# Where a queue's loads stand, and weight sums made by the vector engine, in a hybrid decoder layer

## Chip, core and metric

The kernel runs on one core of a Trainium2 chip. The metric is device time in microseconds (us), the median over runs of the whole program. The engines are named as in the profile: PE is TensorE (matrix products; PEld are its weight loads), DVE VectorE, ACT ScalarE, POOL GpSimd, SP SyncE. SP, ACT and POOL also issue DMA transfers, each from its own in-order instruction stream.

## What is computed

One layer of a decoder over 1,104 tokens (1,040 of a prompt with its 16 meta tokens, 8 sequences of 8 more), model width 1,024. Cut to what matters here:

```
xn = rms_norm(x, gains[0])
u, gate_a, q, f, i, og, m_a, m_b = split(xn @ w_in)           # eight slabs of 1024 columns
y_a = rg_lru(conv(u)) * gelu(gate_a)                          # first recurrent branch
y_b = rms_norm(hgrn2(q, f, i)) * silu(og)                     # second recurrent branch
mixed = sigmoid(m_a) * (y_a @ w_branch_a) + sigmoid(m_b) * (y_b @ w_branch_b)
x = x + rms_norm(mixed @ w_out, gains[1])
x = x + rms_norm(square(relu(rms_norm(x, gains[2]) @ w_up)) @ w_down, gains[3])
```

## The kernel before

All products are made in 16-bit floats with a high and a low part of each operand, three matmuls in place of one. Most weights are multiplied by a seven-product scheme (Strassen-Winograd). A *pair* is two blocks of 128 output channels: 2 x 7 products (the seven for each half of the tokens, `c = 0` and `c = 1`), each of 12 matmuls of 128x272 or 128x276, 168 in all. In the order in which PE makes them the seven use the weight operands S3, S1, A11, S2, A22, S4, A12. The S are sums of the four blocks of a weight matrix; the memory holds the blocks so that each S comes by adding one block to the sum before it.

Each operand is split for use: ACT writes the high part (line 194), DVE the low part (line 196). This *preparation* of the next pair runs between the products of this one: after product i the code calls `tk(i)`, a *tick*, and at the ticks listed in PLACES (c = 0: 1, 3, 5; c = 1: 0, 2, 3, 5; in the second branch c = 0: 0, 1, 2, 3, 5) the generator of the next pair is advanced, before and after `hq.tick`, which advances queued side work after a count of ticks (a *hold*). The engines' instructions stand in exactly the order in which this code emits them.

`gen_pair` makes a pair's operands thus. SP loads blocks 1 and 2 into a tile `ws` (two such tiles, `raw_dma`, line 164) and block 0 into a tile `sa` (two such tiles, `sum_load`, line 182); POOL adds block 1 to `sa` by an accumulating DMA (line 184). The splits are S1 (`sa`), A11 (`ws`), A22 (`ws`), S2, S3, A12, S4. Between them POOL issues three more accumulating DMAs of 256 KB: line 233 (after S1, for S2), line 236 (after A11, for S3), line 242 (after S2, for S4); SP reloads half of `ws` with block 3 (line 239, for A12).

The order of the work around the change: pairs u0 to u7, then gate pairs g3 to g7, then four pairs with `w_branch_b` (the *first branch stage*, operands `ybh`, `ybl`) and four with `w_branch_a` (the *second branch stage*), then `w_out`, then the MLP. The last recurrences run beside u7 to g4. When they are done, `yb_start` hands their memory to new tiles and `y_prep` begins to load the stored parts of y_b on ACT's queue (line 1274), to split them (lines 1280, 1282) and to add them (line 1287) into seven operands numbered 0 to 6, in two halves k = 0 and k = 2; a product of the first branch that needs operand i first forces the rest of that preparation into the order (`ywait`). `th_load` (line 1374, ACT's queue) brings a stored gate slab of 1,088 KB back for a branch pair; the two tiles it uses are those from which g6 and g7 are stored (line 1334, POOL).

In `pair`, line 372 and 380 are ACT's copies after products 1 and 3; line 376 is DVE's `v + b4` after product 2, line 384 `b2 - u` after product 4, line 459 and 460 the differences after product 5. A product that accumulates in or reuses a PSUM bank waits for them: product 6 for line 376, product 2 of the next half for lines 459 and 460.

Of the kernel before, what the change touches and what calls it, by code (L numbers as in the profile page):

```python
# [68 lines left out]
def layer_kernel(ctx, tc, xT, w_pl, w_pr, w_o, w_up, w_dn, gw, par, sconv, slru, shg,  # L69
# [47 lines left out]

    def add_unit(kind, src):
        units.append(kind)
        raws.append(src[:, 1:3] if kind in ("pr", "pn") else src)  # L120
        if kind in ("pr", "pn"):
            prs.append((kind, src))

    npl = npr = 0
# [6 lines left out]
    def add_pair(kind="pr"):  # L131
        nonlocal npr
        add_unit(kind, w_pr[npr])
        npr += 1
# [9 lines left out]
    for _ in range(3):  # L144
        add_pair()
    for s in LSEQ:
        add_pair("pn" if s in NOSTR else "pr")
    for i in range(8):
        add_pair()
        if i >= 4:  # L150
            for j in range(2):
                add_unit("wo", w_o[2 * (i - 4) + j])
    for g in range(NG):
        for src in (w_up, w_dn):
            for i in range(4):
                add_unit("pr", src[4 * g + i])

    st = {"raw": 0, "unit": 0}
    rawq = []
# [8 lines left out]
    def raw_get():  # L168
        if not rawq:
            raw_dma()  # L170
        return rawq.pop(0)
# [5 lines left out]
    def sum_load():  # L177
        if nsum[0] < len(prs):
            kind, src = prs[nsum[0]]
            nsum[0] += 1  # L180
            q = asp.tile([P, 512], F32, tag="sa", name=nm("sa"))
            nc.sync.dma_start(q, src[:, 0])
            if kind == "pr":
                nc.gpsimd.dma_start(q, src[:, 1], accum_op=OP.add)
            sums.append((q, src))

# [11 lines left out]
    def prep(slot=None):  # L198
        kind = units[st["unit"]]
        st["unit"] += 1  # L200
        if slot is None:
            slot = iter(lambda: single(opp), 0)
        ops = {}

        def gen_plain():
            t0 = raw_get()
            ops[0] = next(slot)
            yield from w_split(t0[:, 0], ops[0])
            yield
            ops[1] = next(slot)  # L210
            yield from w_split(t0[:, 1], ops[1])
            raw_dma()

        def gen_wo():
            t0 = raw_get()
            yield from w_split(t0.rearrange("p b (k c) -> p (b k) c", c=P), next(slot))
            raw_dma()
            yield

        def gen_pair():  # L220
            if not sums:
                sum_load()
            q, src = sums.pop(0)
            t0 = raw_get()
            sum_load()
            a, b = t0[:, 0], t0[:, 1]

            def sp(name, x):
                ops[name] = next(slot)
                yield from w_split(x, ops[name])  # L230

            yield from sp("S1", q)
            nc.gpsimd.dma_start(q, src[:, 2], accum_op=OP.add)
            yield
            yield from sp("A11", b)
            nc.gpsimd.dma_start(b, src[:, 0], accum_op=OP.add)
            yield
            yield from sp("A22", a)
            nc.sync.dma_start(a, src[:, 3])
            yield  # L240
            yield from sp("S2", q)
            nc.gpsimd.dma_start(q, src[:, 3], accum_op=OP.add)
            yield
            yield from sp("S3", b)
            yield
            yield from sp("A12", a)
            raw_dma()
            yield
            yield from sp("S4", q)


        def gen_blocks():
            q, src = sums.pop(0)
            t0 = raw_get()
            sum_load()
            a, b = t0[:, 0], t0[:, 1]
            for name, x in (("A22", a), ("A21", q), ("A11", b), ("A12", a)):
                ops[name] = next(slot)
                yield from w_split(x, ops[name])
                if name == "A22":  # L260
                    nc.sync.dma_start(a, src[:, 3])
                if name != "A12":
                    yield
            raw_dma()

        return ops, {"pl": gen_plain, "wo": gen_wo, "pr": gen_pair, "pn": gen_blocks}[kind]()

    cur = {}

# [996 lines left out]

    def y_prep(s, scale, dst, pool, k, ready):
        ks = slice(k, k + 2)  # L1270

        def load(n, tag):
            t = pool.tile([P, 2, HW], F32, tag=f"{tag}{k}", name=nm("ys"))
            nc.scalar.dma_start(t, yb_d[s][n][:, ks])
            return t

        def split(i, t, sc, hold=1):
            hi, lo = (x[:, ks] for x in dst(i))
            yield 0, 1.2, hold
            ACT.activation(hi, t, AF.Copy, scale=sc)  # L1280
            yield 1.3, 0, 1
            DVE.scalar_tensor_tensor(lo, t, sc, hi, op0=OP.mult, op1=OP.subtract)
            ready.add((i, k))

        def add(t, x, hold):
            yield 1.3, 0, hold
            DVE.tensor_tensor(t, t, x, op=OP.add)

        yield 0, 0, 1 + k
        ta, tb = load(4, "yA"), load(3, "yB")  # L1290
        yield from split(5, ta, scale, 8)
        yield 0, 0, 2
        ta = load(0, "yA")
        yield from split(3, tb, scale)
        yield from split(0, ta, scale, 4)
        yield 0, 0, 2
        ta = load(2, "yA")
        yield from add(tb, ta, 6)
        yield from split(4, tb, scale)
        yield from split(2, ta, scale)  # L1300
        yield 0, 0, 2
        ta = load(1, "yA")
        yield from add(tb, ta, 6)
        yield from split(6, tb, scale)
        yield from split(1, ta, -scale)
# [7 lines left out]
    def yb_start():  # L1313
        yield 0, 0, 1
        while hq.has(lrus):
            yield 0, 0, 1
        nc.sync.dma_start(o_conv, convout)
        nc.sync.dma_start(o_h, hout)
        lctx.close()
        ybp = sbuf(ybctx, "ybp", 1, "right")  # L1320
        yb["ysp"] = sbuf(ybctx, "ysp")
        yb["h"] = ybp.tile([P, 7, 4, HW], F16, name="ybh")
        yb["l"] = ybp.tile([P, 7, 4, HW], F16, name="ybl")
        for k in (0, 2):
            ygens[1].append(hq.add(y_prep(1, SY, lambda i: (yb["h"][:, i], yb["l"][:, i]), yb["ysp"], k, yready[1])))

    def ywait(s, i):
        for k in (0, 2):
# [53 lines left out]

    hq.drain([e[0] for e in hq.q if e[0] not in ygens[1]])
    th_load(0)
    th_load(1)

    def ya_start():
        yield 0, 0, 1
        while hq.has(ygens[1]):
            yield 0, 0, 1  # L1390
        for k in (0, 2):
            ygens[0].append(hq.add(y_prep(0, SY / (2 * KAP), lambda i: tuple(x[:, :, :HW] for x in BYa(i)), yb["ysp"], k,
                                          yready[0])))

    for p in range(4):
        tb = ths[p]
# [40 lines left out]
        yield 0, 0, 2  # L1437
        th_load(p)

    def th_late(p):  # L1440
        yield 0, 0, 7
        th_load(p)

    APLACES = ((0, 1, 2, 3, 5), (0, 2, 3, 5))
    ac = acp.tile([P, 2, TO], F32, name="ac")
    for p in range(4):
        if p == 0:
            hq.add(th_late(5))
        if p == 3:
            nc.scalar.dma_start(ac, ac_d[3])  # L1450
        ta = ths[p + 4]
# [566 lines left out]
```

## Time and profile before

| | us |
|---|---|
| median of 3 runs | 1944.09 (1940.73 to 1944.8) |
| profiled execution, its time | 1946.51 |
| its span, first to last instruction | 1944.7 |
| PE busy | 1792.0 (92%) |
| DVE busy | 1397.6 (72%) |
| ACT busy | 998.4 (51%) |
| POOL busy | 448.2 (23%) |

The span is covered by PE for all but 153 us. In the profile's 40 slices of 48.6 us PE stands at 6 to 9 tenths from the 18th to the 27th slice (about 826 to 1313 us) and at 9 tenths in most others; the granted TensorE clock is 0.975 over the whole, and 7 tenths in one slice there. So the stage of the gate pairs and of the two branches is the place to read closely.

### The profile page before, as it was taken

The page shows a single profiled execution, that of the slowest core. Times are in us where ns is not written, and L with a number is a line of the kernel's source. Part 1 is how long each engine was busy: PE and PEld are TensorE (multiplying, and loading weights), DVE is VectorE, ACT ScalarE, POOL GpSimd, SP SyncE. Part 2 cuts the span into 40 slices and gives each one's busy share as a digit, 9 for nine tenths or more (in the row PEclk, how much of TensorE's full clock was granted, in tenths as well). Part 3 has the DMA queues.
Part 4 walks back from the last instruction along what each step waited for, and adds up shares of the span by engine and source line. Part 5 has one row for each costly group of instructions (what it writes and reads, how often), then busy time and mean ns, then how long its engine had stood idle before and what let it go on. Part 6 is the DMA issues. An engine that isn't in the chain of part 4 may idle for free. (4 is left out here: it accounts for less than half of the span.)

```text
span 1944.7 us, 43580 instructions
## 1 busy us (share of the span) xinstructions
PE 1792.0 (92%) x18000; PEld 1532.9 (79%) x18000; DVE 1397.6 (72%) x2615; ACT 998.4 (51%) x2115; POOL 448.2 (23%) x539
## 2 busy tenths in 40 slices
PE   5899999999999999988697869889999999999987
PEld 4788888898888877767476669877888888888776
DVE  7998989888864677756486546687557757756767
ACT  4555545555444666755243334566446426525653
POOL 3512121221221000121022315463111111121222
PEclk9999999999999999999799989999999999999999
DMA  5253333433444233477688853225544544454635
GB/s 177 61 111 77 90 101 80 127 85 88 103 129 123 68 96 95 91 200 201 192 257 219 195 134 93 72 64 106 118 101 103 114 114 100 109 111 102 135 73 163
DMA packets 122809, 232.40 MB, mean 120 GB/s; under 512 B 11632, under 2 KB 49392, under 8 KB 120944
## 3 DMA queue, kind: packets, MB, share of 16 engines
q0 software_dynamic: 46480, 94.88, 25.9%
q1 hardware_dynamic: 62704, 108.52, 17.2%
q10 hardware_dynamic: 13424, 26.19, 4.2%
q8 instruction: 141, 2.31, 0.5%
q14 instruction: 60, 0.49, 0.1%
HBM read 187.92 MB, written 41.63 MB: 118 GB/s over the span
## 5 line engine op out<-in xcount | busy, mean ns | idle before, releaser
L361 PEld LDWEIGHTS <-sh 128*128 128x128 f16 x3968 | 390.7, 98 | 151.8 <-issue 81.6
L362 PEld LDWEIGHTS <-sl 128*128 128x128 f16 x3968 | 390.7, 98 | 85.3 <-DVE sl L196 7.9
L359 PEld LDWEIGHTS <-sh 128*128 128x128 f16 x3968 | 391.5, 99 | 80.0 <-ACT sh L194 7.5
L359 PE MATMUL pd<-xh,sh 128*128 128x276 f16 (+1 forms) x1016 | 285.6, 281 | 12.7 <-DVE et L459 5.0
L361 PE MATMUL pd<-xl,sh 128*128 128x276 f16 (+1 forms) x1016 | 285.5, 281 | 0.0
L362 PE MATMUL pd<-xh,sl 128*128 128x276 f16 (+1 forms) x1016 | 285.3, 281 | 0.0
L359 PE MATMUL q<-aoh,sh 128*128 128x272 f16 (+2 forms) x1008 | 259.5, 267 | 8.2 <-ACT sh L194 5.3
L362 PE MATMUL q<-aoh,sl 128*128 128x272 f16 (+2 forms) x1008 | 259.5, 267 | 3.1 <-DVE sl L196 3.1
L359 PE MATMUL q<-hoh,sh 128*128 128x272 f16 (+2 forms) x952 | 255.4, 273 | 7.3 <-DVE U L1757 4.6
L196 DVE SCALAR_TENSOR_TENSOR sl<-ws,sh 128x512 f16<-128x512 f32 x282 | 193.6, 688 | 91.8 <-ACT sh L194 91.0
L361 PE MATMUL q<-aol,sh 128*128 128x272 f16 (+2 forms) x1008 | 259.5, 267 | 0.0
L362 PE MATMUL q<-hoh,sl 128*128 128x272 f16 (+2 forms) x952 | 255.4, 273 | 1.3 <-DVE sl L196 1.3
L361 PE MATMUL q<-hol,sh 128*128 128x272 f16 (+2 forms) x952 | 255.5, 273 | 0.6 <-DVE hol L1526 0.6
L359 PE MATMUL pd<-tsh,sh 128*128 128x276 f16 (+1 forms) x768 | 218.9, 285 | 30.6 <-DVE U L376 16.7
L196 DVE SCALAR_TENSOR_TENSOR sl<-sa,sh 128x512 f16<-128x512 f32 x189 | 134.1, 711 | 156.7 <-ACT sh L194 155.1
L362 PE MATMUL pd<-tsh,sl 128*128 128x276 f16 (+1 forms) x768 | 219.3, 286 | 0.0
L361 PE MATMUL pd<-tsl,sh 128*128 128x276 f16 (+1 forms) x768 | 219.1, 285 | 0.0
L194 ACT ACTIVATE sh<-ws 128x512 f16<-128x512 f32 x282 | 169.0, 621 | 70.6 <-DMA ws<-in_w_pr 31.6
L194 ACT ACTIVATE sh<-sa 128x512 f16<-128x512 f32 x189 | 117.4, 623 | 147.8 <-DMA sa<-in_w_pr 89.9
L1009 PE MATMUL pd<-sh,xh 128*128 128x128 f16 (+1 forms) x576 | 102.9, 221 | 3.0 <-ACT F L478 2.0
L1011 PE MATMUL pd<-sh,xl 128*128 128x128 f16 (+1 forms) x576 | 102.9, 221 | 0.0
L1010 PE MATMUL pd<-sl,xh 128*128 128x128 f16 (+1 forms) x576 | 102.7, 221 | 0.0
(375 smaller groups left out, 4110.3 us busy)
## 6 DMA issues: line engine op xcount, KB each, us to landing
sa<-in_w_pr POOLq DMA_DIRECT2D x87, 256.0 KB, 4.6
ws<-in_w_pr SPq DMA_DIRECT2D x35, 512.0 KB, 3.9
sa<-in_w_up POOLq DMA_DIRECT2D x48, 256.0 KB, 3.8
sa<-in_w_dn POOLq DMA_DIRECT2D x48, 256.0 KB, 3.8
ys<-yb ACTq DMA_DIRECT2D x20, 544.0 KB, 5.5
sa<-in_w_pr SPq DMA_DIRECT2D x35, 256.0 KB, 3.3
ws<-in_w_pr SPq DMA_DIRECT2D x35, 256.0 KB, 2.9
th<-th ACTq DMA_DIRECT2D x8, 1088.0 KB, 6.6
```

The source lines that it names most:

```text
L194: ACT.activation(hi, src, AF.Copy, scale=SW)
L196: DVE.scalar_tensor_tensor(lo, src, SW, hi, op0=OP.mult, op1=OP.subtract)
L359: PE.matmul(o, h[:, k, :], bh[:, k, c0:c0 + w], start=first and k == 0, stop=False, skip_group_check=not first)
L361: PE.matmul(o, h[:, k, :], bl[:, k, c0:c0 + w], start=False, stop=False, skip_group_check=not first)
L362: PE.matmul(o, l[:, k, :], bh[:, k, c0:c0 + w], start=False, stop=(k == nk - 1), skip_group_check=not first)
L1009: PE.matmul(po, a, wh[:, k % 4, :], start=(k == 0), stop=False)
L1010: PE.matmul(po, a, wl[:, k % 4, :], start=False, stop=False)
L1011: PE.matmul(po, b, wh[:, k % 4, :], start=False, stop=(k == KT - 1))
```

## The change

Two edits of place and one of method.

*Place.* `y_prep` takes its first hold as an argument: 7 ticks in place of 1 where the operands of y_b are made (the other use keeps 1). The second `th_load` is no longer issued with the first one ahead of the first branch, but 7 ticks into it.

*Method.* A new kind of preparation, `gen_half`, stands for 17 pairs: u0, u1, g3 to g7, the eight branch pairs and the first two of `w_up`. The order of splits is A22, S1, A11, S2, A12, S3, S4. The sums for S2 and S4 are DVE additions of 128x512 (lines 270 and 276 of the changed kernel); those for S1 and S3 stay accumulating DMAs on POOL (line 184, and 271 in place of 236).

```
-        raws.append(src[:, 1:3] if kind in ("pr", "pn") else src)
+        raws.append(src[:, 1:3] if kind in ("pr", "pn", "ph") else src)
...
     for s in LSEQ:
-        add_pair("pn" if s in NOSTR else "pr")
+        add_pair("pn" if s in NOSTR else "ph")
     for i in range(8):
-        add_pair()
+        add_pair("ph")
...
+                add_unit("ph" if src is w_up and g == 0 and i < 2 else "pr", src[4 * g + i])
...
-            if kind == "pr":
+            if kind != "pn":
                 nc.gpsimd.dma_start(q, src[:, 1], accum_op=OP.add)
...
+        def gen_half():
...
+            yield from sp("A22", a)
+            nc.sync.dma_start(a, src[:, 3])
+            yield
+            yield from sp("S1", q)
+            yield
+            yield from sp("A11", b)
+            DVE.tensor_tensor(q, q, b, op=OP.add)
+            nc.gpsimd.dma_start(b, src[:, 0], accum_op=OP.add)
+            yield
+            yield from sp("S2", q)
+            yield
+            yield from sp("A12", a)
+            DVE.tensor_tensor(q, q, a, op=OP.add)
+            yield
+            yield from sp("S3", b)
+            raw_dma()
+            yield
+            yield from sp("S4", q)
...
-        yield 0, 0, 1 + k
+        yield 0, 0, hold + k
...
-            ygens[1].append(hq.add(y_prep(1, SY, lambda i: (yb["h"][:, i], yb["l"][:, i]), yb["ysp"], k, yready[1])))
+            ygens[1].append(hq.add(y_prep(1, SY, lambda i: (yb["h"][:, i], yb["l"][:, i]), yb["ysp"], k, yready[1], 7)))
...
     th_load(0)
-    th_load(1)
+
+    def th_late(p, n):
+        yield 0, 0, n
+        th_load(p)
+
+    hq.add(th_late(1, 7))
```

*The first loads of y_b on ACT's queue, in pair g5.* Names: `ys<-yb14`, `ys<-yb13` are the loads, `th` the gate slab of g5, `U_1443` belongs to the second half of g5 and `U_1458` to the first half of g6 (copies of lines 372 and 380, 404 and 412 after), `sh` are the high parts of weights. Before, ACT:

```order
L518 ACTIVATE th_1428_12204<-th_1428_12204 128x276
L518 ACTIVATE th_1428_12204<-pd_1435_12243 128x276
L1274 DMA ys_1441_12344<-yb14_134 128x1088
L1274 DMA ys_1442_12346<-yb13_133 128x1088
L372 ACTIVATE U_1443_12348<-pd_1444_12349 128x276
L194 ACTIVATE sh_1445_12363<-sa_1395_11948 128x512
L1274 DMA ys_1448_12382<-yb14_134 128x1088
L1274 DMA ys_1449_12384<-yb13_133 128x1088
L380 ACTIVATE U_1443_12348<-pd_1450_12386 128x276
L194 ACTIVATE sh_1451_12400<-ws_1388_11865 128x512
```

After, ACT:

```order
L194 ACTIVATE sh_1447_12391<-ws_1388_11865 128x512
L194 ACTIVATE sh_1450_12410<-ws_1388_11865 128x512
L550 ACTIVATE th_1428_12204<-th_1428_12204 128x2x276
L194 ACTIVATE sh_1453_12444<-sa_1395_11948 128x512
L550 ACTIVATE th_1428_12204<-th_1428_12204 128x276
L1306 DMA ys_1455_12448<-yb14_134 128x1088
L1306 DMA ys_1456_12450<-yb13_133 128x1088
L550 ACTIVATE th_1428_12204<-pd_1446_12377 128x276
L404 ACTIVATE U_1458_12467<-pd_1459_12468 128x276
L1306 DMA ys_1460_12482<-yb14_134 128x1088
L1306 DMA ys_1461_12484<-yb13_133 128x1088
```

The loads moved from the middle of g5 (ahead of its copies U of c = 1) to its end, two of the four to behind the first copy U of g6.

*The start of the first branch on ACT's queue.* `th<-th0` and `th<-th1` are the gate slabs, `U_1521` (before) and `U_1518` (after) the copies of its first half pair, `ys<-yb11` the last two loads of y_b, `ybh` high parts of its operands. Before, ACT:

```order
L1274 DMA ys_1514_12923<-yb11_131 128x1088
L1280 ACTIVATE ybh_12327<-ys_1492_12741 128x1088
L518 ACTIVATE th_1489_12725<-th_1489_12725 128x2x276
L194 ACTIVATE sh_1516_12958<-sa_1463_12501 128x512
L518 ACTIVATE th_1489_12725<-th_1489_12725 128x276
L518 ACTIVATE th_1489_12725<-pd_1508_12887 128x276
L1274 DMA ys_1518_12976<-yb11_131 128x1088
L1374 DMA th_1519_12979<-th0_135 128x2176
L1374 DMA th_1520_12981<-th1_136 128x2176
L372 ACTIVATE U_1521_12983<-pd_1522_12984 128x272
L194 ACTIVATE sh_1525_13015<-sa_1494_12757 128x512
L380 ACTIVATE U_1521_12983<-pd_1527_13020 128x272
```

After, ACT:

```order
L1406 DMA th_1517_12971<-th0_135 128x2176
L404 ACTIVATE U_1518_12973<-pd_1519_12974 128x272
L194 ACTIVATE sh_1522_13006<-ws_1484_12666 128x512
L412 ACTIVATE U_1518_12973<-pd_1524_13012 128x272
L1306 DMA ys_1525_13026<-yb11_131 128x1088
L1312 ACTIVATE ybh_12326<-ys_1502_12844 128x1088
L194 ACTIVATE sh_1527_13043<-sa_1492_12749 128x512
L1312 ACTIVATE ybh_12326<-ys_1456_12450 128x1088
L1306 DMA ys_1529_13051<-yb11_131 128x1088
L1312 ACTIVATE ybh_12326<-ys_1461_12484 128x1088
L1312 ACTIVATE ybh_12326<-ys_1525_13026 128x1088
L194 ACTIVATE sh_1532_13088<-ws_1484_12666 128x512
```

The load of `th1` left the place ahead of the copies, and the two loads of `yb11` came from ahead of it to behind the second copy U, the second of them behind a split of operand 6.

*The same place on DVE:* `ys_1456<-ys_1456,ys_1525` (line 1319) adds the load of `yb11` into operand 6, line 408 and 416 are `v + b4` and `b2 - u` of the first half. After, DVE:

```order
L408 TENSOR_TENSOR U_1518_12973<-U_1518_12973,pd_1520_12989 128x272
L1314 SCALAR_TENSOR_TENSOR ybl_12327<-ys_1461_12484,ybh_12326 128x1088
L196 SCALAR_TENSOR_TENSOR sl_1523_13007<-ws_1484_12666,sh_1522_13006 128x512
L416 TENSOR_TENSOR U_1518_12973<-pd_1526_13029,U_1518_12973 128x272
L1314 SCALAR_TENSOR_TENSOR ybl_12327<-ys_1502_12844,ybh_12326 128x1088
L196 SCALAR_TENSOR_TENSOR sl_1528_13044<-sa_1492_12749,sh_1527_13043 128x512
L1319 TENSOR_TENSOR ys_1456_12450<-ys_1456_12450,ys_1525_13026 128x1088
L1314 SCALAR_TENSOR_TENSOR ybl_12327<-ys_1456_12450,ybh_12326 128x1088
L1319 TENSOR_TENSOR ys_1461_12484<-ys_1461_12484,ys_1529_13051 128x1088
L1314 SCALAR_TENSOR_TENSOR ybl_12327<-ys_1461_12484,ybh_12326 128x1088
```

Before, DVE:

```order
L376 TENSOR_TENSOR U_1521_12983<-U_1521_12983,pd_1523_12998 128x272
L196 SCALAR_TENSOR_TENSOR sl_1526_13016<-sa_1494_12757,sh_1525_13015 128x512
L1287 TENSOR_TENSOR ys_1442_12346<-ys_1442_12346,ys_1514_12923 128x1088
L384 TENSOR_TENSOR U_1521_12983<-pd_1528_13035,U_1521_12983 128x272
L196 SCALAR_TENSOR_TENSOR sl_1530_13050<-ws_1485_12673,sh_1529_13049 128x512
L1282 SCALAR_TENSOR_TENSOR ybl_12328<-ys_1442_12346,ybh_12327 128x1088
L1287 TENSOR_TENSOR ys_1449_12384<-ys_1449_12384,ys_1518_12976 128x1088
L1282 SCALAR_TENSOR_TENSOR ybl_12328<-ys_1449_12384,ybh_12327 128x1088
```

The sum of operand 6 stands at the same place in both; the load that it reads stands later on ACT's queue.

*POOL around the first pair of the second branch stage* (`sa<-in_w_pr` are lines 184, 233, 242, `ws<-in_w_pr` is line 236, 271 after, `th<-ac` merges the two branches). Before:

```order
L1378 DMA ac3_146<-th_1613_13649 128x2176
L184 DMA sa_1668_14083<-in_w_pr 128x512
L233 DMA sa_1631_13791<-in_w_pr 128x512
L236 DMA ws_1664_14049<-in_w_pr 128x512
L1418 DMA th_1648_13908<-ac0_143 128x2x272 x2
L242 DMA sa_1631_13791<-in_w_pr 128x512
L1418 DMA th_1648_13908<-ac0_143 128x2x272 x2
L184 DMA sa_1703_14342<-in_w_pr 128x512
```

After:

```order
L1410 DMA ac3_146<-th_1613_13649 128x2176
L184 DMA sa_1668_14083<-in_w_pr 128x512
L1455 DMA th_1648_13908<-ac0_143 128x2x272
L271 DMA ws_1664_14049<-in_w_pr 128x512
L1455 DMA th_1648_13908<-ac0_143 128x2x272 x3
L184 DMA sa_1703_14342<-in_w_pr 128x512
```

Of three accumulations per pair that follow the first, one is left, and one merge transfer now stands ahead of it.

## Rows read from the trace of the kernel before

**Rows 1.** Busy time by stretch; columns as in its first row.
```profile
core 0: us, PE busy (x) PEld busy (x) DVE busy (x) ACT busy (x) POOL busy (x), PEclk, DMA share, GB/s
860.00:922.00 62.00, 52.32 (x423) 41.93 (x422) 33.03 (x53) 28.22 (x52) 11.31 (x14) 0.97 0.79 227
922.00:960.00 38.00, 18.41 (x103) 12.37 (x103) 17.29 (x25) 10.62 (x17) 3.28 (x4) 0.64 0.57 166
960.00:1037.00 77.00, 71.39 (x607) 59.17 (x606) 60.35 (x98) 34.07 (x55) 12.89 (x16) 1.00 0.85 252
1037.00:1153.00 116.00, 83.99 (x661) 66.79 (x661) 66.50 (x122) 36.69 (x67) 31.81 (x32) 0.92 0.82 196
960.00:980.00 20.00, 20.00 (x175) 16.89 (x174) 14.51 (x26) 7.93 (x14) 4.00 (x5) 1.00 0.84 264
```

**Rows 2.** PE's waits, second branch stage: total, times, longest.
```profile
PE pd L359 <- DVE U L376: 16.7, 4, 5.3
PE pd L359 <- DVE th L550: 3.8, 2, 2.7
```

**Rows 3.** Line 233, 960 to 1153: who waited, and landing times.
```profile
  ACT sh L194: 45.0, 7
DMA to landing us min/median/max: 6.0/8.1/9.2
```

**Rows 4.** Line 242, same stretch: landing times.
```profile
DMA to landing us min/median/max: 3.8/5.3/8.4
```

**Rows 5.** Line 236, same stretch: landing times.
```profile
DMA to landing us min/median/max: 8.2/8.8/10.3
```

**Rows 6.** Timeline, first pair of the second branch stage: start, duration, engine, idle before.
```profile
1038.90 0.33 SPq L164 DMA_DIRECT2D ws<-in_w_pr  x1
1044.96 0.63 ACT L194 ACTIVATE sh<-ws 128x512 f16<-128x512 f32 x1 [6.55 <-DMA ws<-in_w_pr]
1046.72 0.28 PE L359 MATMUL pd<-xh,sh 128*128 128x272 f16 x1 [1.81 <-DVE et L459]
1047.42 0.86 POOL L184 DMA_DIRECT2D sa<-in_w_pr  x1 [8.82 <-DMA sa<-in_w_pr]
1048.50 1.55 POOL L236 DMA_DIRECT2D ws<-in_w_pr  x1
1056.11 0.63 ACT L194 ACTIVATE sh<-sa 128x512 f16<-128x512 f32 x1 [9.72 <-DMA sa<-in_w_pr]
1057.87 0.39 PE L359 MATMUL pd<-tsh,sh 128*128 128x272 f16 x1 [5.32 <-DVE U L376]
```

**Rows 7.** ACT's timeline around its two long waits.
```profile
869.92 0.40 ACT L372 ACTIVATE U<-pd 128x276 f32<-128x276 f32 x1 [7.19 <-DMA out_o_h<-hout]
922.26 1.09 ACT L1280 ACTIVATE ybh<-ys 128x1088 f16<-128x1088 f32 x1
926.19 11.61 ACTq L1374 DMA_DIRECT2D th<-th  x2
937.84 0.40 ACT L372 ACTIVATE U<-pd 128x272 f32<-128x272 f32 x1 [11.30 <-DMA th<-th]
```

**Rows 8.** PE's timeline: gate pair, start of the first branch stage.
```profile
870.38 0.28 PE L359 MATMUL pd<-tsh,sh 128*128 128x276 f16 x1 [4.39 <-ACT U L372]
...
922.97 0.28 PE L359 MATMUL pd<-ybh,sh 128*128 128x272 f16 x1 [1.05 <-DVE U L384]
...
941.87 0.38 PE L359 MATMUL pd<-ybh,sh 128*128 128x272 f16 x1 [13.10 <-ACT ybh L1280]
...
947.73 0.43 PE L362 MATMUL pd<-ybh,sl 128*128 128x272 f16 x1
```

**Rows 9.** Line 1274, loads of y_b: landing times.
```profile
DMA to landing us min/median/max: 3.7/5.8/9.6
```

**Rows 10.** DVE groups by shape, 860 to 1153: count, busy us, mean ns.
```profile
L1282 DVE SCALAR_TENSOR_TENSOR ybl<-ys,ybh 128x1088 f16<-128x1088 f32 x14 | 17.9, 1288 | 5.8 <-ACT ybh L1280 5.8
L1287 DVE TENSOR_TENSOR ys<-ys,ys 128x1088 f32<-128x1088 f32 x8 | 10.3, 1283 | 0.0
L1427 DVE TENSOR_TENSOR th<-th,ac 128x544 f32<-128x544 f32 x1 | 0.7, 726 | 0.0
```

More of the change, by code (lines that the diff above doesn't have):

```diff
@@ L119, in add_unit @@
         units.append(kind)
-        raws.append(src[:, 1:3] if kind in ("pr", "pn") else src)
-        if kind in ("pr", "pn"):
+        raws.append(src[:, 1:3] if kind in ("pr", "pn", "ph") else src)
+        if kind in ("pr", "pn", "ph"):
             prs.append((kind, src))
@@ L155, in layer_kernel @@
             for i in range(4):
-                add_unit("pr", src[4 * g + i])
+                add_unit("ph" if src is w_up and g == 0 and i < 2 else "pr", src[4 * g + i])
     st = {"raw": 0, "unit": 0}
@@ L249, in gen_pair, with sp @@
             yield from sp("S4", q)
+        def gen_half():
+            if not sums:
+                sum_load()
+            q, src = sums.pop(0)
+            t0 = raw_get()
+            sum_load()
+            a, b = t0[:, 0], t0[:, 1]
+            def sp(name, x):
+                ops[name] = next(slot)
+                yield from w_split(x, ops[name])
+            yield from sp("A22", a)
[16 more added lines that the diff above has]
+            yield from sp("S4", q)
         def gen_blocks():
@@ L264, in gen_blocks @@
             raw_dma()
-        return ops, {"pl": gen_plain, "wo": gen_wo, "pr": gen_pair, "pn": gen_blocks}[kind]()
+        return ops, {"pl": gen_plain, "wo": gen_wo, "pr": gen_pair, "pn": gen_blocks, "ph": gen_half}[kind]()
     cur = {}
@@ L1265, in lru, with y_prep @@
             nc.gpsimd.dma_start(yb_d[0][4][:, k], yb, accum_op=OP.add)
-    def y_prep(s, scale, dst, pool, k, ready):
+    def y_prep(s, scale, dst, pool, k, ready, hold):
         ks = slice(k, k + 2)
@@ L1392, in ya_start @@
             ygens[0].append(hq.add(y_prep(0, SY / (2 * KAP), lambda i: tuple(x[:, :, :HW] for x in BYa(i)), yb["ysp"], k,
-                                          yready[0])))
+                                          yready[0], 1)))
     for p in range(4):
@@ L1438, in th_next @@
         th_load(p)
-    def th_late(p):
-        yield 0, 0, 7
-        th_load(p)
     APLACES = ((0, 1, 2, 3, 5), (0, 2, 3, 5))
@@ L1447, in layer_kernel @@
         if p == 0:
-            hq.add(th_late(5))
+            hq.add(th_late(5, 7))
         if p == 3:
```

## Prediction

> **What bounds the kernel now.** I read the profile's page for the stage in which PE is not full, then the busy times of that stage in four stretches, then who PE waited for in each, and last the timelines of the longest waits. A full stretch gives the unit: 175 matmuls in 20.00 us at clock 1.00, 0.1143 us each [rows 1], so a product of 12 is 1.37 us and a pair of 168 is 19.2 us. At that rate the gate pairs from 860 to 922 (423 matmuls of 276 columns, at 276/272 of it, 49 us) lose 13 of 62 us; the start of the first branch stage (103, 12 us) loses 26 of 38; the rest of that stage (607, 69.4 us) loses 7.6 of 77. From 1037 to 1153 PE stands idle 32.0 of 116 us, and its 83.99 busy us for 661 matmuls are at least 8.4 more than they need at full rate, at a mean clock of 0.92 [rows 1].
>
> Three kinds of wait make this. First, ACT stands twice in front of a DMA that it cannot issue yet: 7.19 us until the recurrence's last store has left the memory which the loads of y_b reuse, and 11.30 us until g7's slab has been stored out of the tile into which the second `th_load` goes [rows 7]. PE then waits 4.39 and 13.10 us [rows 8]. Second, in a branch pair the split for S2 comes at the first tick of c = 1, while its accumulating DMA (line 233) needs 8.1 us to land and is issued behind the next pair's first sum, which waits for its own load: ACT waits 45.0 us for it in seven cases [rows 3]. DVE's low part stands behind ACT's, line 376 behind that, and product 6 waits: 16.7 us in four cases in the second branch stage [rows 2]. Third, S4 (line 242, landing 3.8 to 8.4 us [rows 4]) holds `th` of line 550 and PE once for 2.7 us [rows 2].
>
> **The change part by part.** *ACT's first wait.* The loads now stand six ticks later, 8.2 us at 1.37. ACT had passed the place of the first wait at 869.92 [rows 7], and one half pair (9.6 us) after the old place the store has landed, so nothing is waited for. PE's 4.39 us and the lower pace behind them go, and S2's waits in g4 to g7 too. Of the 13 us I take 8; bounds 4.4 and 11.
>
> *ACT's second wait, and what is late next.* ACT's 11.30 us go: the second `th_load` now stands some 20 us into the first branch stage. But with the hold the last two loads of y_b (for operands 6 and 1) also move: before they were issued ahead of `th_load`, after they stand behind the second copy U of the first branch pair, and the second of them behind the split of operand 6's first half. Counted from that stage's first matmul: product 3 ends at 4.1 us, the copy at 4.5, the load goes out at 4.6 and lands 5.8 later (median of rows 9) at 10.4; the addition of 1.28 [rows 10] ends at 11.7. Only then ACT passes the split of 1.09 [rows 7] and issues the second load, which lands at 17.5; addition 18.8, high part 19.9, low part (1.29, rows 10) 21.2, and the last six matmuls of product 5, at half clock twice the unit each, end at 22.6. Before, product 5 ended 25.2 us after the first matmul: 947.73 + 0.43 - 922.97 [rows 8]. So of the 13.10 us and its sequel only 2.6 are won. ACT arrives about 2 us late there because S3 of g7's preparation (below) holds it. I take 1. With both loads at 3.7 or both at 9.6 us [rows 9] it is +5 or -7.
>
> A rule speaks against this edit: the Trainium skill, DMA: Bandwidth & Descriptors, section Rules for kernel authors, says to issue a transfer early, compute, and wait for it late; this hold does the reverse for the last two loads. The trace agrees so far as its loads, issued early, cost PE nothing of their own there before ACT's queue stopped. By that rule this place loses; it is a rival below.
>
> *The additions on DVE.* 34 of 128x512. No such row stands in the trace; the nearest is 0.726 us for 128x544 [rows 10], so 0.69 each, 23 us of DVE in all. In the second stage DVE is busy 66.50 of 116 us, 8 additions (5.5 us) lie beside the stretches in which it waited for ACT; cost 0 to 5.5, I take 1. In the rest of the first branch stage DVE is busy 60.35 us against 69.4 us of PE work; 3.6 pairs bring 5.0 us, to 65. It is then nearly as full as PE. The two S2 waits there and part of the small ones go, but DVE gives no slack: of the 7.6 us lost I take 2 as won (bounds -3 and 6).
>
> *The order of the splits.* A22 now comes first and needs the `ws` tile, where S1 came first and did not. In the second branch stage that tile's load is issued one tick before: 1038.90, landed 1044.96, PE held until 1046.72 by line 459 [rows 6]. After it, two low parts and line 384 stand ahead of line 459 where one low part did, about 1 us; in three of four pairs, 3 us.
>
> *S3.* Its accumulating DMA (line 236) was issued after the second split and needed at the fifth; now it is issued after the third split and an addition and needed at the sixth. It lands 8.2 to 10.3 us after issue [rows 5]. In the first pair of the second branch stage: before, line 236 went out at 1048.50 [rows 6] behind two others; now A11 takes the time of A22, the addition follows, and it goes out near 1050.5. With landing time L, high part, low part and line 459 end near 1050.5 + L + 2.0. PE needs line 459 at product 2 of the next pair: 1046.72 + 1 + 7 x 1.37 = 1057.3. PE's wait is L - 4.8. For L the bounds are 3.8, an accumulation with little ahead of it [rows 4], and 10.3; nearest is 8.8, the same transfer at the same place [rows 5], with one 256 KB accumulation fewer ahead of it but one merge transfer more: I take 7.0. That is 2.2 us a pair, 8.8 in four. In gate and first branch pairs the `ws` load is early: product 6 ends at 8.2 us, splits and addition make the issue near 10.5, line 459 ends at 12.5 + L, and the need is at 15 x 1.37 = 20.6: nothing is lost up to L = 8.1.
>
> *Second branch stage, summed.* Gone: 16.7 for S2, 2.7 for S4 [rows 2], and of the 8.4 at low clock 7 (two waits at its end stay): 26.4. Taken back: 3 + 8.8 + 1. Net 13.6.
>
> u0, u1 and the two `w_up` pairs I price at nothing: their S2 waits there are short or lie in the second stage's sum already; POOL loses two issues a pair there, under other work.
>
> **Sum:** 8 + 1 + 2 + 13.6 = 25 us. The profiled execution took 1946.51 us (1.8 beside its span of 1944.7) and would take 1921.5; it lies 2.4 above the median of the runs, 1944.09, which would become 1919. I predict 1920.
>
> **The rivals.**
> *S3 becomes the wait, slower.* One mechanism: the one accumulation left lands as late as it did at worst. Everything that doesn't hang on L is worth 8 + 1 + 2 + (26.4 - 3 - 1) = 33.4 us. L takes back 4 (L - 4.8), and in nine gate and first branch pairs L - 8.1 above 8.1. At 8.8 that is 22.3, at 10.3 it is 41.8: 8 us more than is won, 1955 by the profiled time. It decides from L = 9.7 on, above which the kernel is slower. For it: 10.3 stands in the trace. Against: three accumulations became one per pair. Chance 0.09.
> *The loads of y_b come too late.* Both take 9.6 us and product 5 ends 8 us later than forecast; the DVE work behind it (line 459, low parts) delays the next pair too. Gain 25 - 8 - 3 = 14, time 1932. For it: `ywait` forces the two loads one after the other. Chance 0.17; with an S3 at L = 8.8 besides (13.5 us less) nothing is left of the gain.
> *Nothing is given back, faster.* S3 lands in 5 us (0.8 us taken back in all, not 8.8), both y_b loads in 3.7: 25 + 8 + 4, and 4 more if DVE's queue in the first branch stage keeps up: 41, 1905. For it: of four accumulations a pair two are gone. Against: the stores of 1,088 KB and the merges stay on that queue. Chance 0.13.
> *DVE takes PE's place in both branch stages*, or the y_b loads and S3 together eat the gain: within 4 us of before. Chance 0.09; DVE's 66.50 + 5.5 of 116 us speaks against it.
>
> **How the numbers follow.** My forecast, gains of 17 to 34 us, has 0.52. About 0.2% (4 us) is what a measurement of this kernel can tell from no change. Faster: 0.52 + 0.17 + 0.13 = 0.82; same 0.09; slower 0.09. The range leaves out the slower case, most of the case of no change and the far end of the largest gain: 1902 to 1940.
>
> **What would show it.** Right: no wait of ACT for `out_o_h` or for the second `th_load`; no wait of PE for line 408 (was 376) with S2 behind it in the second branch stage; PE's wait at product 5 of the first branch pair still there in two pieces of 5 to 7 us, released by `ybh`, with a lower clock behind it; ACT's waits in branch pairs now for `ws` (line 271), the landing near 7 us; PE's waits there on line 491 (was 459), 2 to 3 us a pair. Wrong: line 271 landing at 9 us or more; DVE without gaps in the first branch stage while PE waits; a wait of ACT for the loads of y_b at their new first place.

## The result, and the profile after

The changed kernel took 1927.8 us (median of four runs, 1922.5 to 1929.2), the one before beside it 1942.4 (1938.4 to 1944.8): ratio 0.9922, 95% interval 0.9895 to 0.9948, so 14.6 us faster. The forecast was 1920, its range 1902 to 1940. The profiled run after took 1922.5 us (span 1920.7), the fastest of its four; the one before 1946.5, above all of the four. So the two profiles lie 24.0 us apart, more than the change brings, and below a second profile of the same kernel stands beside the first.

Busy time by stretch, columns as in [rows 1], but cut at the first matmuls of the stages: from the second half of g5 to the first branch stage, its first half pair, the rest of it, the second branch stage.

```profile
855.74:910.70 54.96, 51.61 (x423) 41.48 (x420) 33.69 (x58) 26.26 (x49) 6.44 (x8) 0.97 0.73 221
910.70:944.30 33.60, 14.05 (x87) 9.48 (x85) 20.77 (x26) 12.33 (x17) 2.44 (x3) 0.70 0.54 176
944.30:1018.36 74.06, 70.41 (x590) 58.14 (x589) 59.53 (x98) 32.58 (x52) 6.80 (x9) 0.98 0.72 228
1018.36:1122.63 104.27, 85.13 (x674) 67.23 (x672) 68.01 (x124) 37.13 (x66) 24.75 (x23) 0.95 0.80 195
```

The same four cuts of the kernel before:

```profile
860.18:922.97 62.79, 52.14 (x422) 41.79 (x420) 33.82 (x55) 29.19 (x53) 11.16 (x13) 0.97 0.79 225
922.97:956.14 33.17, 14.55 (x84) 9.76 (x84) 15.88 (x22) 8.75 (x14) 3.28 (x4) 0.64 0.64 188
956.14:1031.86 75.72, 70.67 (x589) 58.27 (x588) 55.72 (x91) 31.63 (x52) 12.89 (x16) 0.98 0.82 246
1031.86:1144.97 113.11, 86.40 (x674) 68.40 (x672) 65.97 (x119) 37.57 (x68) 31.78 (x31) 0.92 0.84 201
```

The first and the last stretch became shorter by 7.8 and 8.8 us, the first half pair of the first branch stage not at all. Span less PE busy is PE's idle time: in the last stretch it fell from 26.7 to 19.1 us, while the busy time of the same 674 matmuls fell only by 1.3.

PE's waits in the second branch stage of the changed kernel (total, times, longest), which answer to [rows 2]:

```profile
PE pd L391 <- ACT sh L194: 7.9, 2, 4.6
PE pd L391 <- DVE U L416: 7.9, 4, 3.6
```

For line 271, S3's accumulating DMA, who waited from 944 to 1130 and the landing times; they answer to [rows 5]:

```profile
  ACT sh L194: 27.1, 5
DMA to landing us min/median/max: 3.7/4.9/9.8
```

These seven cases are of both branch stages and of the first `w_up` pair. The three for pairs 2 to 4 of the second branch stage, before (line 236) and after:

```profile
DMA to landing us min/median/max: 8.2/8.6/8.8
DMA to landing us min/median/max: 4.9/8.1/9.5
```

S2's waits (line 376, now 408; 16.7 us) are gone. Two others stand in their place: S3's high part itself, and the subtraction of b2 on DVE (line 416). Before, PE had waits on line 459 too, which [rows 2] does not show; the changed kernel has none on that line (now 491):

```profile
PE pd L359 <- DVE et L459: 5.0, 4, 1.8
```

To compare stages over all kernels I read the start of each half pair from PE's timeline. In us: the start of g3; the stretch from there to the first branch stage (gates); that stage's first half pair (b0a) and its rest; the second branch stage (a); from there to the end; then the timed median and its ratio to the kernel before.

| kernel | g3 at | gates | b0a | rest | a | to the end | timed | ratio (95%) |
|---|---|---|---|---|---|---|---|---|
| before | 800.8 | 122.1 | 33.2 | 75.7 | 113.1 | 799.7 | 1942.4 | 1 |
| changed | 795.6 | 115.1 | 33.6 | 74.1 | 104.3 | 798.1 | 1927.8 | 0.9922 (0.9895, 0.9948) |
| after_again | 796.5 | 115.0 | 35.3 | 77.4 | 103.0 | 800.6 | 1928.2 | 0.9931 (0.9916, 0.9946) |
| place_only | 795.9 | 119.5 | 38.1 | 71.8 | 114.7 | 797.6 | 1941.3 | 1.0008 (0.9993, 1.0023) |
| method_only | 797.8 | 113.3 | 33.9 | 72.4 | 106.6 | 799.9 | 1929.3 | 0.9934 (0.9918, 0.9950) |
| hold1_late | 795.1 | 111.6 | 22.5 | 73.1 | 106.4 | 799.1 | 1915.1 | 0.9861 (0.9841, 0.9881) |
| hold4_late | 797.4 | 113.4 | 28.7 | 74.0 | 103.8 | 804.1 | 1921.1 | 0.9881 (0.9863, 0.9900) |
| th_only | 800.5 | 122.9 | 23.8 | 74.1 | 113.2 | 800.2 | 1932.5 | 0.9949 (0.9934, 0.9964) |
| s3_fifth_h1 | 795.4 | 117.7 | 23.0 | 76.8 | 112.7 | 801.2 | 1926.4 | 0.9916 (0.9900, 0.9931) |
| a22_third_h1 | 794.5 | 116.4 | 22.2 | 71.7 | 103.5 | 806.2 | 1922.5 | 0.9891 (0.9871, 0.9912) |
| old_order_h1 | 795.5 | 117.0 | 22.7 | 72.0 | 101.7 | 805.2 | 1915.8 | 0.9859 (0.9844, 0.9873) |
| a_early | 794.4 | 111.6 | 24.1 | 77.2 | 103.5 | 800.3 | 1915.2 | 0.9866 (0.9849, 0.9883) |
| b_early | 796.6 | 117.6 | 23.1 | 73.4 | 99.2 | 805.8 | 1914.0 | 0.9861 (0.9840, 0.9882) |
| b_early_old | 795.5 | 116.3 | 22.5 | 71.2 | 99.0 | 804.6 | 1912.5 | 0.9860 (0.9838, 0.9883) |

A stage of one profile is good to 2 or 3 us: two profiles of the changed kernel differ by 0.1, 1.7, 3.3 and 1.3. The last column is worse: hold4_late runs the same code there as the changed kernel and takes 804.1 beside 798.1 and 800.6. The medians were taken in several sessions, with 1940.0 to 1942.6 us for the kernel before, so kernels are best compared by their ratios. Before and th_only reach g3 5 us later than place_only, although all three run the same code up to there: that part of the 24 us is no effect of the change.

### The profile page after: what moved, and what is told of

It reads as the page before. It is cut to its first block, busy times and chain, and to the rows that moved or that the text cites. A ratio compares the mean times of both kernels' runs of the same rounds, so it can differ in the third digit from the quotient of the medians.

```text
span 1920.7 us, 43520 instructions
## 1 busy us (share of the span) xinstructions
PE 1786.6 (93%) x18000; PEld 1526.8 (79%) x18000; DVE 1418.6 (74%) x2649; ACT 1000.1 (52%) x2115; POOL 417.5 (22%) x505
## 5 line engine op out<-in xcount | busy, mean ns | idle before, releaser
L391 PEld LDWEIGHTS <-sh 128*128 128x128 f16 x3968 | 391.1, 99 | 92.3 <-ACT sh L194 19.9
L1665 PE MATMUL q<-mh,woh 128*128 128x144 f16 (+1 forms) x512 | 95.8, 228 | 6.8 <-ACT mh L1458 5.9
```

The lines of the kernel that those rows point to most:

```text
L391: PE.matmul(o, h[:, k, :], bh[:, k, c0:c0 + w], start=first and k == 0, stop=False, skip_group_check=not first)
L1665: PE.matmul(ps[:, :w], wo[j][0][:, k, :], mh[:, k, t0:t0 + w], start=(k == 0), stop=False)
```

## Experiments

**The changed kernel again.** No edit.

> The changed kernel once more, to see how far its profile and times lie apart from run to run. The four times so far are 1922.5 to 1929.2; the profile shown is of the fastest. Expected: 1924 to 1930, ratio 0.990 to 0.994; a profile whose second branch stage is 104 to 107 us. If the profile's 8.8 us there were chance of one run, it would be 108 or more.

1928.2 us, ratio 0.9931, its profile 7.2 us longer than the first. The second branch stage is 103.0 us, below the 104 to 107 expected, so the gain there is no chance of one run.

**The places alone, the sums alone.** place_only is the kernel before with

```diff
-        yield 0, 0, 1 + k
+        yield 0, 0, hold + k          # 7 for the second branch's y_b
...
-    th_load(1)
+    hq.add(th_late(1, 7))
```

and method_only the changed kernel without these two places.

> The kernel before with the two new places alone (loads of y_b six ticks later, second th_load seven ticks into the first branch stage); the weight sums stay four DMAs a pair. My theory (the sums of weights bring most, of the places only the first one does): the gate half pair of the first ACT wait (g5 second half) goes from 16.1 to about 10 us, the first half pair of the first branch stage stays at 33 to 34 us because the last loads of y_b are now what comes late there, the second branch stage stays near 113 us; total 4 to 8 us less than before. Rival, the places bring the gain: 12 us less than before or more. Rival, the places only pay together with the new sums: within 3 us of before.

> The changed kernel with both loads back at their old places; only the weight sums are new. My theory: the second half of g5 is back at about 16 us and the first half pair of the first branch stage stays long (33 us or more), the second branch stage stays near 104 us; total 8 to 11 us less than before, so 4 to 7 more than the changed kernel. Rival, the places bring the gain: at most 3 us less than before, second branch stage above 110.

Together the two places bring nothing (1.0008, where I expected 4 to 8 us), and the sums alone as much as the whole change (1929.3 beside 1928.2), more than the 8 to 11 us that I expected of them. The second half of g5 became shorter with the places alone (16.1 to 10.0 us), as my theory had it, but this was handed back in two halves further on and in the first half pair of the first branch stage (38.1 us). Rows of place_only, ACT, DVE and PE in g6, and PE at the two halves of product 5 of the first branch pair:

```profile
884.55 0.63 ACT L194 ACTIVATE sh<-sa 128x512 f16<-128x512 f32 x1 [6.63 <-DMA sa<-in_w_pr]
885.82 0.43 DVE L376 TENSOR_TENSOR U<-U,pd 128x276 f32<-128x276 f32 x1
886.31 0.39 PE L359 MATMUL pd<-xh,sh 128*128 128x276 f16 x1 [3.19 <-DVE U L376]
...
934.18 0.38 PE L359 MATMUL pd<-ybh,sh 128*128 128x272 f16 x1 [7.35 <-ACT ybh L1280]
943.34 0.39 PE L359 MATMUL pd<-ybh,sh 128*128 128x272 f16 x1 [6.54 <-ACT ybh L1280]
```

With S2 still summed by a DMA, ACT that no longer waits for the recurrence's store meets S2 instead (6.63 us), and g6's and g7's second halves take 14.8 us each. In method_only ACT's wait for the store is back (6.5 us, PE 3.67), and yet its gate pairs are the shorter ones, 113.3 us. In the changed kernel the place still takes g5's second half from method_only's 15.4 us to 9.9, but g6 and g7, four halves of 9.9 in method_only, take 10.4, 12.7, 12.0 and 9.9 there, and the first half of g4 15.7 beside 14.0. So in net the 8 us that I gave to this place came from the sums.

**The start of the first branch stage.** hold1_late and hold4_late are the changed kernel with the y_b loads' hold at 1 (as before) and 4:

```diff
-            ygens[1].append(hq.add(y_prep(1, SY, lambda i: (yb["h"][:, i], yb["l"][:, i]), yb["ysp"], k, yready[1], 7)))
+            ygens[1].append(hq.add(y_prep(1, SY, lambda i: (yb["h"][:, i], yb["l"][:, i]), yb["ysp"], k, yready[1], 1)))
```

th_only is the kernel before with the second `th_load` late and nothing else.

> The changed kernel with the loads of y_b at their old place, the second th_load still late: the pair of loads for operands 6 and 1 again stands ahead of the first branch stage. My theory (in the changed kernel those loads' lateness has taken the place of ACT's wait for g7's store): first half pair of the first branch stage falls from 33.6 to 20 to 25 us, ACT's 7 us wait for the recurrence's store returns and g5's second half is again near 16 us; total 2 to 6 us less than the changed kernel. Rival (g7's preparation on ACT and DVE is what is late there, not the loads): the half pair stays at 31 to 34 us, total 4 to 7 us more than the changed kernel.

> The changed kernel with the loads of y_b three ticks later than before instead of six. In its program order the first load for operands 6 and 1 stands ahead of the first branch stage's th_load by 5 rows and the second behind it; with six ticks both stand behind, with none both ahead. My theory (the first half pair of the first branch stage follows these two loads): between the 22.5 us of none and the 33.6 of six, 26 to 30; total 1919 to 1925. Rival (a cliff at one place): 22 to 24 or 32 to 34.

> The kernel before with the second th_load late and nothing else. My theory (the place of the second th_load is worth what the changed kernel gives back through the later loads of y_b): first half pair of the first branch stage from 33.2 to 21 to 25 us, all other stages as before, total 1930 to 1936. Rival (the load's wait only hides the lateness of y_b or of g7's splits): half pair 31 us or more, total within 3 us of before.

My theory of the half pair held in all three. hold1_late's total gained 13 us where I expected 2 to 6, since its g6 and g7 run without a wait as well and g5's second half takes 13.7 us, not 16. So one of the two places gains and the other loses: the late `th_load` is worth 14 us with the sums (method_only to hold1_late) and 9.5 without them (th_only), and the late loads of y_b cost 13 (hold1_late to after_again), all timed. ACT's queue and one DVE addition in the changed kernel, from the first matmul at 910.70:

```profile
917.30 0.33 ACTq L1306 DMA_DIRECT2D ys<-yb  x1
...
925.64 1.29 DVE L1319 TENSOR_TENSOR ys<-ys,ys 128x1088 f32<-128x1088 f32 x1 [3.67 <-DMA ys<-yb]
926.96 1.11 ACT L1312 ACTIVATE ybh<-ys 128x1088 f16<-128x1088 f32 x1 [7.66 <-DVE ys L1319]
926.97 0.33 ACTq L1306 DMA_DIRECT2D ys<-yb  x1
...
931.23 1.29 DVE L1319 TENSOR_TENSOR ys<-ys,ys 128x1088 f32<-128x1088 f32 x1 [1.83 <-DMA ys<-yb]
932.56 1.11 ACT L1312 ACTIVATE ybh<-ys 128x1088 f16<-128x1088 f32 x1 [4.48 <-DVE ys L1319]
```

PE's rows for it, still of the changed kernel:

```profile
928.12 0.38 PE L391 MATMUL pd<-ybh,sh 128*128 128x272 f16 x1 [8.51 <-ACT ybh L1312]
933.72 0.39 PE L391 MATMUL pd<-ybh,sh 128*128 128x272 f16 x1 [2.98 <-ACT ybh L1312]
941.85 0.38 PE L393 MATMUL pd<-ybl,sh 128*128 128x272 f16 x1 [3.30 <-DVE ybl L1314]
```

The same places of hold1_late, where both loads stand ahead of the stage, and ACT's wait in g5:

```profile
862.37 0.40 ACT L404 ACTIVATE U<-pd 128x276 f32<-128x276 f32 x1 [6.25 <-DMA out_o_h<-hout]
...
918.57 0.39 PE L391 MATMUL pd<-ybh,sh 128*128 128x272 f16 x1 [2.93 <-ACT ybh L1312]
926.75 0.39 PE L393 MATMUL pd<-ybl,sh 128*128 128x272 f16 x1 [3.30 <-DVE ybl L1314]
```

In the changed kernel the waits of [rows 7] are gone, and for the 13.10 us of [rows 8] stand 8.51 and 2.98; the 3.30 in product 7 is in hold1_late too. The addition of operand 6 stands one product later in DVE's order than before, behind `b2 - u` (line 416) and not, as the section on the change has it, at the same place; it waits 3.67 us for its load all the same. The chain load, addition, split, load, addition, split is what PE waits for in the changed kernel; take the hold away and 11 to 13 us of that half pair go, at the price of ACT's 6.25 us for the store, which cost PE 3.46. The three holds 1, 4, 7 give 22.5, 28.7, 33.6 us: with 4 one load stands ahead of the stage and one in it. The Trainium skill, DMA: Bandwidth & Descriptors, section Rules for kernel authors, says to issue a transfer early and to wait for it late; these runs agree for the loads of y_b, by 13 us between hold 1 and hold 7. They do not for the second `th_load`: issued later it gained 9.5 us (th_only), since early it held ACT's queue until its tile was free.

**The second branch stage: which split is late.** Three kernels on hold1_late, each with another order of the splits in `gen_half`; in all the two additions stay on DVE.

```
 hold1_late    A22, S1, A11, S2, A12, S3, S4
 s3_fifth_h1   A22, S1, A11, S2, S3, A12, S4
 a22_third_h1  S1, A11, A22, S2, A12, S3, S4
 old_order_h1  S1, A11, A22, S2, S3, A12, S4
```

> Same base, only S3 goes ahead of A12 (fifth); A22 stays first. My theory: the waits for S3's high part at the starts of pairs shrink to 0 to 2 us, those for the subtraction of b2 stay; stage 97 to 102 us, total 1906 to 1911. Rival (S3's accumulating DMA is not landed at the fifth place either): ACT waits the more there, A12 and S4 come late behind it, stage 106 or more, total 1915 or more.

> Same base, only A22 (and its reload with A12) is moved back from first to third; S3 stays sixth. My theory: the waits for the subtraction of b2 at second halves go (some 8 us in four pairs), the waits for S3's high part at the starts of pairs stay at 2 to 5 us; stage 97 to 102 us, total 1906 to 1911. Rival (A22 is not what is late): stage within 2 us of 106.4.

> The kernel with the loads of y_b early and the second th_load late, and the splits of a half-summed pair in the old order S1, A11, A22, S2, S3, A12, S4, the two additions still on DVE. Its base has 106.4 us in the second branch stage, with waits of 2.9 to 5.3 us at the starts of pairs for S3's high part and of 0.8 to 4.2 us at the starts of second halves for the subtraction of b2 on DVE. My theory (A22 first holds ACT and DVE at the ws load, and S3 sixth is late for the next pair's first product): both kinds go, stage at 92 to 98 us, total 1900 to 1906. Rival (the accumulating DMA of S3 lands late whatever its place; a fifth split that waits for it only holds A12 and S4 as well): stage at 104 or more, total 1913 or more.

S3 fifth is the rival's outcome: stage 112.7 us, 6.3 longer, and PE waits 19.9 us in six for line 416. ACT stands at S3 and everything behind it on ACT and DVE is late. A22 third brought 2.9 us where I expected 4 to 9, hardly more than two profiles differ by, and its total is 7 us above its base where I expected 4 to 9 below (0.9891 beside 0.9861, the intervals overlap a little). Both changes together, which by the first result should lose, gave the shortest stage of the three, 101.7 us (I expected 92 to 98); but the old order takes 5.4 us more in the gate pairs and 6.1 after the stage, and the total is the same. Of the 6.1, 2 us are PE's wait for the last merged part before the output projection (7.65 us beside 5.60 in hold1_late); the rest is within what that column varies by. So moving either split does not end the lateness. The changed kernel's rows show why; the first five show the preparation of the second pair, the last five that of the third:

```profile
1025.11 0.33 SPq L164 DMA_DIRECT2D ws<-in_w_pr  x1
...
1031.57 0.63 ACT L194 ACTIVATE sh<-ws 128x512 f16<-128x512 f32 x1 [7.45 <-DMA ws<-in_w_pr]
1032.23 0.69 DVE L196 SCALAR_TENSOR_TENSOR sl<-ws,sh 128x512 f16<-128x512 f32 x1 [5.67 <-ACT sh L194]
1032.84 0.43 DVE L416 TENSOR_TENSOR U<-pd,U 128x272 f32<-128x272 f32 x1
1033.33 0.39 PE L391 MATMUL pd<-xh,sh 128*128 128x272 f16 x1 [3.61 <-DVE U L416]
...
1059.37 0.68 DVE L196 SCALAR_TENSOR_TENSOR sl<-ws,sh 128x512 f16<-128x512 f32 x1
1059.97 0.68 DVE L270 TENSOR_TENSOR sa<-sa,ws 128x512 f32<-128x512 f32 x1
1061.20 0.91 POOL L271 DMA_DIRECT2D ws<-in_w_pr  x1 [1.49 <-DVE th L582]
1069.37 0.63 ACT L194 ACTIVATE sh<-ws 128x512 f16<-128x512 f32 x1 [6.41 <-DMA ws<-in_w_pr]
1070.06 0.29 PE L391 MATMUL pd<-xh,sh 128*128 128x272 f16 x1 [3.28 <-ACT sh L194]
```

A22's load takes 6.5 us and is issued at 1025.11; ACT, DVE's low part and behind it the subtraction that frees PE's bank wait for it. For the third pair the chain goes on: A11's low part and the addition, only then S3's DMA at 1061.20 (its row names line 582, the next instruction on DVE), 8.2 us to the high part, and PE's first product of the next pair waits for that directly.

**Taking the load's wait away.** a_early is hold1_late with an own tile for A22 of pairs 2 to 4, loaded a pair earlier; b_early and b_early_old do the same for A11's block on a22_third_h1 and old_order_h1.

```diff
+            if unit in early:
+                a = ax.pop()              # b = bx.pop() in b_early
...
             yield from sp("A12", a)       # S3, b in b_early
             DVE.tensor_tensor(q, q, a, op=OP.add)
+            if unit in early:
+                ax_load(unit + 3)
```

> The kernel with the loads of y_b early and the second th_load late, and in the second branch stage the block A22 of pairs 2 to 4 has a tile of its own, loaded right after the pair before has split A12 instead of one tick before its own split; line 164 loads only the other half. My theory (A22, now first, waits for a load that is issued one tick ahead; DVE's low part and the subtraction of b2 stand behind it): the waits of PE for line 416 at second halves, 4.2, 1.5, 0.8 and 1.2 us, go, those for S3's high part become shorter but stay above 1 us; stage from 106.4 to 97 to 101 us, total 1906 to 1911. Rival (ACT only meets the next late transfer, A11's half, one split further): stage 104 or more, total within 3 us of 1915.

> Base is the kernel with the loads of y_b early, the second th_load late and the splits S1, A11, A22, S2, A12, S3, S4 (1922.5 us; its second branch stage 103.5 us). Added: in the second branch stage A11's block of pairs 2 to 4 has a tile of its own, loaded right after the pair before has split S3, so neither A11 nor the accumulating DMA of S3 behind it waits for the late load; line 164 loads only A22's half. My theory (what is left in that stage is S3: its DMA is issued late and lands after 7 to 10 us): it goes out one split earlier, PE's waits at the starts of pairs shrink from 1.4 to 3.7 us to under 1, stage 95 to 100 us, total 1913 to 1919. Rival (ACT meets A22's half late instead, DVE's queue behind it): stage 102 or more, total within 3 us of its base.

> The same tile for A11, with the splits in the old order S1, A11, A22, S2, S3, A12, S4 (base 1915.8 us, second branch stage 101.7 us). My theory: the load no longer delays A11, S3 has 8 us from issue to its split, stage 94 to 99 us, total 1908 to 1913; a gain in the stage above 3 us may be lost again where PE waits for the last merge before the output projection, 7.7 us in the base. Rival (the landing of S3, not its issue, is what is late): stage 101 or more, total 1915 or more.

In a_early PE's waits for line 416 (here 435) at the second halves of the first three pairs went, as my theory said, and one of 2.2 us was left; the stage gained only 2.9 us where I expected 5 to 9, and the total nothing, because S3 came out behind them. PE's waits (total, times, longest) in the stage:

```profile
PE pd L410 <- ACT sh L208: 12.4, 3, 5.5
PE pd L410 <- DVE U L435: 2.2, 1, 2.2
```

The line of S3's DMA in the same kernel, who waited and the landing times:

```profile
  ACT sh L208: 26.3, 4
DMA to landing us min/median/max: 3.7/9.5/10.2
```

With A11 early instead, the stage fell by 4.3 us (b_early) and 2.7 (b_early_old), to 99 us, though PE still waits 2.3 to 3.9 us at the starts of three pairs in b_early, where I expected less than 1; the ratios are 0.9861 (base 0.9891, the intervals overlap a little) and 0.9860 (base 0.9859), and neither total can be told from hold1_late's 0.9861. In b_early_old PE's waits left are again on the subtraction of b2, with ACT now at S3:

```profile
PE pd L410 <- DVE U L435: 11.4, 3, 4.3
PE pd L410 <- DVE et L510: 1.3, 1, 1.3
```

And S3's DMA there:

```profile
  ACT sh L208: 24.5, 4
DMA to landing us min/median/max: 5.8/8.0/9.7
```

So in this stage two transfers, the plain load of a pair's blocks and S3's accumulation, are late by similar amounts, and removing the wait for one shows the other. I did not shorten S3's landing itself (a third addition on DVE would need one more tile), so how far the stage falls without both stays open; at the full rate of [rows 1] its 674 matmuls need 77.0 us.

## Why the prediction was right, and where its sizes were off

The direction and the range were right, and so were the three causes of waiting. The forecast of 1920 was 8 us too low, mainly by one term, the time expected back from the low clock. Two others, the gate pairs and S3's wait, came out nearly right for another reason than mine, which is luck.

*Gate pairs, +8.* Measured 7.1 (both profiles after). The size was right, its ground was not: I had put it mainly to the loads' new place. place_only and method_only show that place to be worth 2.6 us without the sums and -1.8 with them, no more than two profiles differ by, and the sums worth 8.8 us without the place. The 7.1 holds losses that I had priced at nothing: the first half of g4 takes 15.7 us (12.6 before), and g7's first product waits for S3's high part, which landed after 9.0 us there, above my 8.1:

```profile
888.79 0.29 PE L391 MATMUL pd<-tsh,sh 128*128 128x276 f16 x1 [2.71 <-ACT sh L194]
```


*Start of the first branch stage, +1.* Measured -0.4 and -2.1. The step was right: the 11.30 us for g7's slab went and the two last loads took its place. Its times were a little short: the first load went out 6.6 us after the first matmul, not 4.6, its addition began 8.3 us later (I took 5.8; [rows 9] has up to 9.6), the second load went out 16.3 us after the first matmul. Product 5 ended at 25.6 us, not 22.6 (25.2 before). That the hold by itself loses at this place, which I had as a rival, is what hold1_late shows.

*Rest of that stage, +2.* Measured +1.6 and -1.7, so nothing that two profiles can show. The assumption that S3 costs nothing here was wrong: PE's timeline of the changed kernel has a wait for its high part there, behind a landing of 9.8 us:

```profile
977.08 0.29 PE L391 MATMUL pd<-ybh,sh 128*128 128x272 f16 x1 [3.33 <-ACT sh L194]
```

*Second branch stage, 13.6.* Measured 8.8 and 10.1. This is the step with the wrong size, and it is one term of it: the 7 of 8.4 us that I expected back from the low clock. PE's idle time should have fallen by 16.7 + 2.7 - 3 - 8.8 - 1 = 6.6 us; it fell by 7.6 in the changed kernel and 9.7 in its second profile. PE's busy time should have fallen by 7 and fell by 1.3 and 0.4 (86.40 to 85.13 and 86.04, at a mean clock of 0.95 and 0.93 instead of 0.92). Waits were still there, at other places, and the clock stayed below full rate with them.

*Inside it, the places of the new waits.* The two that I priced, A22 first and S3 late, are the ones that came, 7.9 us each in all. For S3 8.8 was forecast; for A22 3 on top of line 459's own 5.0, which are gone, so 8.0. But I had put them on line 459 (now 491). S3's high part is used by the next pair's first product, so PE waits for that and not for a later accumulation; A22's delay reaches PE through the subtraction of b2, which stands behind its low part in DVE's queue. In this stage S3 landed after 4.9, 8.1 and 9.5 us, 7.5 in the mean, beside the 7.0 that I took. My L - 4.8 gives 0.1, 3.3 and 4.7 for these, and PE waited 0, 3.28 and 4.65. That it fits so well is luck: the need comes one product (1.37 us) earlier than I had it, and the low part and line 459, some 1.3 us, fall out of the chain.

*The additions, 0.69 us each.* 0.684 for both lines. DVE was no bound: 68.01 busy of 104.27 us.

*u0, u1 and the `w_up` pairs, nothing.* The changed kernel reaches g3 at 795.6 and 796.5 us, place_only, where u0 and u1 are as before, at 795.9.

*The rivals and the signs.* Of the loads' lateness 3 of the rival's 8 us came. S3 as the wait came true in kind, 7.9 us, below the 9.7 us of landing at which it decides. The signs of being right came (no wait of ACT for the recurrence's store or at the second `th_load`, none of PE with S2 behind it, product 5 in two pieces, 8.51 and 2.98 us) but for the waits on line 491; one sign of being wrong came in part, line 271 landing after 9.5 and 9.8 us in two of seven cases. Over the stages, the mean of the two profiles after gives 7.1 - 1.3 + 0 + 9.5 and 0.4 behind the stage, 15.7 us, beside 14.6 timed.

## What to carry to other kernels

A wait that is removed is worth what the next late thing leaves of it: list, for the same engine and stretch, what stands behind it in order, and when each could be ready. A transfer that is held back until its memory is surely free saves a blocked queue but starts its own chain later; where another load was the real blocker (here the second `th_load`), move only that one. And do not count low-clock time to the gain where waits are left: here PE's idle time in the second branch stage fell by 7.6 us, and of 9.4 us over the full rate 8.1 stayed.

## What had not been expected of the hardware

Between the kernel before and the changed one PE's idle time in the second branch stage fell by 7.6 us, but the matmuls' own excess over the full rate (86.40 and 85.13 against 77.0 us) only from 9.4 to 8.1 (9.0 in its second profile); in s3_fifth_h1, with 23.1 us idle of 112.7, it was 12.6 at a mean clock of 0.89.

The same accumulating transfer of 256 KB landed after 3.7 to 9.8 us, although two of four accumulations a pair were gone. Over both branch stages the median fell (8.8 [rows 5] to 4.9), but among the second branch stage's own three only from 8.6 to 8.1, and the longest there rose from 8.8 to 9.5. What decides between 4 and 10 us no run here shows.
